# One SSD staging buffer at another address of the arena: over RWKV head pairs 3 and 4 instead of over pairs 5 to 7

## The chip, the cores and the metric

The kernel runs on one core of a Trainium2 chip. The metric is the device time of one execution in microseconds (us). The times and the profile are of the hardware. TensorE is called PE here, its weight loads PEld, VectorE DVE, ScalarE ACT, GpSimd POOL, and SyncE, which issues most of the loads, SP.

## The reference

One layer over 256 tokens of width 1024, in float32:

```
h = LN(x)
z, xbc, dt, f_rwkv, f_hgrn, gates = split(h @ w_in)
y_a = SSD(z, conv(xbc), dt)        16 heads of 64, 2 groups, state 128, chunks of 64
y_b = RWKV7(f_rwkv)                16 heads of 64, delta-rule state
y_c = HGRN2(f_hgrn)                8 heads of 128
m   = sum_i sigmoid(gate_i) * (y_i @ w_br_i)
h   = LN(alpha*h + m @ w_out)
h   = LN(alpha*h + MoE(h))         16 experts of 512, top 2 of one group of 4
```

For the SSD, the columns x, b and c of xbc are convolved along time and go through SiLU. Then, for each group, the products of c and b over the tokens are multiplied by decay factors, and these weights are multiplied with x.

## The kernel before

The 256 tokens are held as two tiles of 128. All of the mixers' scratch lies in one SBUF tile, the *arena*, of 122 KB on each partition. A `Bump` hands out pieces of it between two addresses in KB, and a named piece is a ring of buffers that is used over and over. Nothing is copied or freed when a stage takes over addresses of an earlier one: the program puts a wait on whatever read or wrote these bytes last. A scheduler orders the instructions of each engine when the program is built, by its own model of durations and by which instruction could start; every engine then runs its list strictly in that order. A different address can so change the order on all engines.

The stages, as the program writes them:

- `rwkv_part` and `rwkv_a` prepare the RWKV heads in pairs p = 0 to 7. Pair p keeps its chunk matrices at 8 + 9.5p KB: first `bkt` (2 KB), `uv` (2 KB), `sc` (4 KB), `ars` (1.5 KB). Pair 3 lies at 36.5 to 46, pair 4 at 46 to 55.5, pair 5 at 55.5 to 65, pair 6 at 65 to 74.5, pair 7 at 74.5 to 84.
- `rwkv_b` runs the recurrence over four chunks for two pairs at a time, in four rounds j = 0 to 3; round 3 is pairs 6 and 7. One chunk is a chain of small matmuls (L654, L658, L662, L670) with ACT copies between them, and the round ends with L687 and L691, which read `uv`, `sc` and `ars` for the last time. Then follow a group norm on DVE (L694 to L708), transposes (L717) and the output (L722 to L724). `hgrn(j)` stands beside each round; its last transposes are L920, of what ACT writes in L917.
- `feat` multiplies the normalized input with 256 columns of `w_in`. `stream` loads the weights by SP into `raw`, splits them on ACT (`whi`, L183) and DVE (`wlo`, L184) into two parts, and PE runs 48 matmuls of 128x256 (L366, L367, L368), 12 for one split tile; four split tiles can be ahead of PE. These *streams* are most of PE's work, and the scheduler puts them between the small matmuls. A stream with `yhi`, `ylo` instead of `hhi`, `hlo` is that of a branch, whose input y is split by the same two lines.
- `ssd_prep` convolves b and c (`conv`, L928 to L933) into `bcm`, with the ring `cth` as scratch, and multiplies them (L1003, L1004) into the products `cb` of the two groups.
- `ssd_weights(g)` loads the decay sums `ab` by a DMA that POOL issues (L1020), for token tile 0 and, into the same buffer, for tile 1. ACT makes `wdg` of each with eight Relus (L1029) and an Exp (L1031), and `woff` of the second with an Exp (L1023); DVE multiplies them by `cb` (L1032, L1024).
- `ssd` transposes x (L1064), scales it on DVE (L1067, L1069) and multiplies with the three weights: L1073 with `wdg` of tile 0, L1075 with `wdg` of tile 1, L1077 with `woff`.
- `branches`, `router` and `moe` follow. The MoE weights are loaded by SP into slots of the arena as these come free.

Of the kernel before, what the change touches and what calls it, by code (L numbers as in the profile page):

```python
# [139 lines left out]
class Kern:  # L140
# [847 lines left out]
    def ssd_prep(self):  # L988

        nc, A = self.nc, self.A  # L990
        mp = self.pmm
        a = self.sda = Bump(self.ar, 64, 102)
        bcm = a.new([128, 4, L])
        for m in range(2):
            ps = self.feat(COL_B + m * 256)
            for f in range(2):
                th = a.new([128, L], "cth", 2)
                self.conv(ps[:, f, :], 8 + 2 * m + f, bcm[:, 2 * m + f, :], th)
        self.gates(range(NG - NZ - NY, NG - NZ))
        self.cbs = []  # L1000
        for g in range(2):
            cps = mp.tile([128, 3, 128], F32, name="mm")
            nc.tensor.matmul(cps[:, 0:2, :], bcm[:, g, 0:128], bcm[:, 2 + g, :], start=True, stop=True)  # L1003
            nc.tensor.matmul(cps[:, 2, :], bcm[:, g, 128:256], bcm[:, 2 + g, 128:256], start=True, stop=True)  # L1004
            cb = a.new([128, 3, 128])
            nc.vector.tensor_tensor(cb[:, 0:3:2, :], cps[:, 0:3:2, :],
                                    self.tri[:, None, :].to_broadcast([128, 2, 128]), op=OP.mult)
            nc.scalar.activation(cb[:, 1, :], cps[:, 1, :], AF.Copy)
            self.cbs.append(cb)
# [721 lines left out]
```

## Time and profile before

| what | value |
|---|---|
| median of 3 runs | 830.43 us (830.31 to 831.64) |
| profiled execution | 829.69 us |
| span of that execution, first to last instruction | 827.9 us |
| PE busy | 784.8 us, 95% of the span |
| DVE, ACT, POOL busy | 510.1, 369.7, 134.7 us |
| mean granted clock of PE | 0.977 of full speed |

The profiled execution is 0.7 us below the median of the runs. A busy share of an engine is the time in which at least one of its instructions ran; the time between the span and the execution's time (1.8 us) lies before the first and after the last instruction.

### The profile page before, as it was taken

How to read it: one execution, taken by the hardware profiler on the slowest of the kernel's cores; microseconds unless marked ns; L12 is line 12 of the kernel's file. 1: busy time of each engine (PE TensorE's matmuls, PEld its weight loads, DVE VectorE, ACT ScalarE, POOL GpSimd, SP SyncE). 2: the span in 40 equal slices, each digit the busy share in tenths (PEclk: the TensorE clock that was granted, in tenths of full speed). 3: DMA queues.
4: the chain of work that ended last, by engine and by line, in shares of the span. 5: the costliest groups of instructions: out<-in, count | busy, mean ns of one | idle time of the engine just before them, and what ended most of it. 6: DMA issues, size and time to landing. Idle time of an engine off the chain costs nothing. (4 is left out here: it accounts for less than half of the span.)

```text
span 827.9 us, 16484 instructions
## 1 busy us (share of the span) xinstructions
PE 784.8 (95%) x6354; PEld 604.5 (73%) x6354; DVE 510.1 (62%) x1150; ACT 369.7 (45%) x824; POOL 134.7 (16%) x204
## 2 busy tenths in 40 slices
PE   7999969999999999999998999999999999999991
PEld 5898859988898899898797999999444434443440
DVE  6897669999997555567579887785611111111136
ACT  3755445574645555645477755453412121211111
POOL 3364614450102001102002111000000000001201
PEclk9999969999999999999899999999999999999996
DMA  7544564575445455366179568985999999999941
GB/s 229 177 118 114 50 161 119 140 180 155 107 132 148 128 155 153 103 203 193 38 237 299 178 205 283 349 271 161 390 386 386 387 387 386 387 386 386 386 179 54
DMA packets 146526, 183.93 MB, mean 222 GB/s; under 512 B 25609, under 2 KB 94472, under 8 KB 146440
## 3 DMA queue, kind: packets, MB, share of 16 engines
q1 hardware_dynamic: 142888, 176.91, 65.3%
q0 software_dynamic: 1504, 3.20, 2.2%
q10 hardware_dynamic: 2048, 2.70, 1.0%
q8 instruction: 52, 0.85, 0.4%
q14 instruction: 34, 0.28, 0.1%
HBM read 180.12 MB, written 2.65 MB: 221 GB/s over the span
## 5 line engine op out<-in xcount | busy, mean ns | idle before, releaser
L183 ACT ACTIVATE whi<-raw 128x512 fp32r<-128x512 f32 x268 | 165.5, 623 | 162.9 <-PE st L367 126.3
L184 DVE TENSOR_TENSOR wlo<-raw,whi 128x512 fp32r<-128x512 f32 x268 | 189.1, 715 | 77.3 <-ACT whi L183 64.2
L368 PE MATMUL st<-hhi,wlo 128*128 128x256 f32 (+1 forms) x744 | 212.0, 293 | 9.0 <-DVE wlo L184 8.8
L366 PE MATMUL st<-hhi,whi 128*128 128x256 f32 (+1 forms) x744 | 210.0, 290 | 2.2 <-ACT arena L784 1.4
L367 PE MATMUL st<-hlo,whi 128*128 128x256 f32 (+1 forms) x744 | 208.4, 288 | 0.0
L368 PEld LDWEIGHTS st<-hhi,wlo 128*128 128x128 f32 (+1 forms) x744 | 140.3, 192 | 16.6 <-DVE wlo L184 10.8
L366 PEld LDWEIGHTS st<-hhi,whi 128*128 128x128 f32 (+1 forms) x744 | 140.5, 192 | 7.1 <-issue 2.6
L367 PEld LDWEIGHTS st<-hlo,whi 128*128 128x128 f32 (+1 forms) x744 | 140.3, 192 | 3.1 <-issue 1.6
L1445 PE MATMUL b<-arena,xg 128*64 128x512 f32 x288 | 78.8, 596 | 0.0
L367 PE MATMUL st<-ylo,whi 128*128 128x256 f32 x192 | 53.8, 288 | 1.5 <-DVE ylo L184 1.5
L366 PE MATMUL st<-yhi,whi 128*128 128x256 f32 x192 | 53.9, 287 | 0.0
L368 PE MATMUL st<-yhi,wlo 128*128 128x256 f32 x192 | 53.1, 287 | 0.4 <-DVE wlo L184 0.2
L1445 PEld LDWEIGHTS b<-arena,xg 128*64 128x64 f32 x288 | 23.9, 137 | 38.0 <-issue 34.5
L1515 DVE SCALAR_TENSOR_TENSOR elo<-b,egs,ehi 128x512 fp32r<-128x512 f32 x15 | 11.3, 750 | 60.7 <-ACT ehi L1514 60.7
L1495 PE MATMUL b<-arena,ehT 128*64 128x512 f32 x144 | 43.0, 596 | 0.0
L367 PEld LDWEIGHTS st<-ylo,whi 128*128 128x128 f32 x192 | 36.4, 192 | 2.1 <-DVE ylo L184 1.7
L368 PEld LDWEIGHTS st<-yhi,wlo 128*128 128x128 f32 x192 | 36.2, 193 | 1.0 <-DVE wlo L184 0.8
L366 PEld LDWEIGHTS st<-yhi,whi 128*128 128x128 f32 x192 | 36.5, 192 | 0.3 <-ACT yhi L183 0.2
L1360 POOL TENSOR_TENSOR arena<-arena 128x512 f32<-128x512 bf16 x4 | 4.5, 1158 | 197.2 <-PE b L1445 197.2
L1484 ACT ACTIVATE ehT<-b 128x256 f32<-128x256 f32 x16 | 6.2, 389 | 67.7 <-PE b L1483 67.7
L1476 DVE SCALAR_TENSOR_TENSOR ehi<-ehi,b 128x256 f32<-128x256 f32 x16 | 6.0, 418 | 47.2 <-PE b L1445 47.2
L593 DVE TENSOR_TENSOR arena<-arena 128x1 f32<-128x1 f32 (+15 forms) x64 | 34.0, 531 | 0.8
(448 smaller groups left out, 1431.0 us busy)
## 6 DMA issues: line engine op xcount, KB each, us to landing
raw<-in_w_in_dram SPq DMA_DIRECT2D x102, 512.0 KB, 3.8
arena<-in_exp_w_gate_dram SPq DMA_DIRECT2D x40, 512.0 KB, 10.8
arena<-in_exp_w_down_dram SPq DMA_DIRECT2D x34, 512.0 KB, 10.8
arena<-in_exp_w_up_dram SPq DMA_DIRECT2D x32, 512.0 KB, 10.8
xsl<-in_exp_w_up_dram SPq DMA_DIRECT2D x32, 512.0 KB, 10.8
xsl<-in_exp_w_down_dram SPq DMA_DIRECT2D x20, 512.0 KB, 10.8
xsr<-in_exp_w_gate_dram SPq DMA_DIRECT2D x16, 512.0 KB, 10.8
raw<-in_w_br_rwkv_dram SPq DMA_DIRECT2D x8, 512.0 KB, 4.0
```

The costliest lines, as they stand in the source:

```text
L183: nc.scalar.activation(hi, raw, AF.Copy)
L184: nc.vector.tensor_tensor(lo, raw, hi.bitcast(F32), op=OP.subtract)
L366: nc.tensor.matmul(o, hi[:, kq, fs], xhi[:, k, :], start=st and f == 0, stop=False)
L367: nc.tensor.matmul(o, hi[:, kq, fs], xlo[:, k, :], start=False, stop=False)
L368: nc.tensor.matmul(o, lo[:, kq, fs], xhi[:, k, :], start=False, stop=sp and f == nf - 1)
L593: nc.vector.tensor_tensor(po, tu[:, :n, :t + 1], eu[:, :t + 1, t][:, None, :].to_broadcast([128, n, t + 1]), op=OP.mult)
L1360: nc.gpsimd.tensor_tensor(o, x[1], x[2], op=OP.add)
L1445: nc.tensor.matmul(ps[hs[e]], xg[:, k, hs[e]], W[nm, e, k // 2][:, k % 2, :], start=k == 0, stop=k == KT - 1)
L1476: nc.vector.scalar_tensor_tensor(th[:, c], th[:, c], 0.5, q["pu"][:, c], op0=OP.mult, op1=OP.mult)
L1484: nc.scalar.activation(q["hT"][:, 2 * j:2 * j + 2], tp, AF.Copy)
L1495: nc.tensor.matmul(pd[hs[e], :], q["hT"][:, k, hs[e]], W["exp_w_down", e, (n, k // 2)][:, k % 2, :], start=k == 0, stop=k == 3)
L1515: nc.vector.scalar_tensor_tensor(lo, pd, q["gs"], hi.bitcast(F32), op0=OP.mult, op1=OP.subtract)
```

## The change

`bcm`, `cth` and the two `cb` are taken from a Bump at 40 to 49 KB (9 KB are exactly what they need). They had come from the SSD's Bump at 64 KB, in which everything that `ssd_weights` and `ssd` take after them now moves down: `ab` from 73 to 64, the first `wdg` from 77 to 68, `woff` from 81 to 72, the second `wdg` from 85 to 76. `ssd` takes its own `cth` from that Bump.

```diff
@@ -989,7 +989,8 @@
 
         nc, A = self.nc, self.A
         mp = self.pmm
-        a = self.sda = Bump(self.ar, 64, 102)
+        self.sda = Bump(self.ar, 64, 102)
+        a = Bump(self.ar, 40, 49)
         bcm = a.new([128, 4, L])
         for m in range(2):
             ps = self.feat(COL_B + m * 256)
```

The added line moves every later line of the file down by one, so that L1020 of before is L1021 now, and so on. The order of the instructions changes from round 1 of the recurrence on. Three places matter below.

On PE, in round 3 of the recurrence (pairs 6 and 7), before: the second chunk follows the first, and the third the second, with no stream between.

```order
L368 MATMUL st<-hhi,wlo 128x256
L654 MATMUL ch<-arena 64x64 x2
L658 MATMUL ch<-arena 64x64 x2
L654 MATMUL ch<-arena 64x64 x2
L658 MATMUL ch<-arena 64x64 x2
L662 MATMUL ch<-arena 64x64 x4
L670 MATMUL ch<-arena 64x64 x4
```

The same place on PE now, up to the first streams behind that step; 19 stream matmuls stand there before the chunk's L662.

```order
L654 MATMUL ch<-arena 64x64 x2
L658 MATMUL ch<-arena 64x64 x2
L654 MATMUL ch<-arena 64x64 x2
L658 MATMUL ch<-arena 64x64 x2
L368 MATMUL st<-hhi,wlo 128x256
L366 MATMUL st<-hhi,whi 128x256 x2
L367 MATMUL st<-hlo,whi 128x256 x2
```

Streams stand now between all the steps of round 3. When the last L691 of round 3 is reached, PE has 2098 stream matmuls behind it before the change and 2197 now, of 3192 in all; the other matmuls up to there are as many (831 before it in both).

On PE, behind that last L691, now: 35 stream matmuls (not shown), and then the head of the SSD.

```order
L715 MATMUL ch<-arena 128x256 x2
L920 MATMUL mm<-ident,hr 128x128
L1004 MATMUL mm<-arena 128x256
L1005 MATMUL mm<-arena 128x128
L920 MATMUL mm<-ident,hr 128x128
L717 MATMUL ch<-ident,arena 128x128 x4
L920 MATMUL mm<-ident,hr 128x128 x2
L1004 MATMUL mm<-arena 128x256
L1005 MATMUL mm<-arena 128x128
L1065 MATMUL mm<-ident,arena 128x128 x2
L366 MATMUL st<-yhi,whi 128x256
L1074 MATMUL mm<-arena 64x128 x2
```

Two more L1065, 12 stream matmuls of the branch, and the ten matmuls L1076, L1078, L1074, L1076, L1078 follow at once. Before the change, 169 stream matmuls stand between the last L691 and the last of these ten; now 48 do. PE has 2267 stream matmuls behind it at that last matmul (L1077 before, L1078 now) before the change and 2245 now.

On ACT, at the same place, now: the group norm's squares (L703), the last two splits for the 35 streams, and then the SSD's weights in one run.

```order
L703 ACTIVATE arena<-arena 128x256 x2
L183 ACTIVATE whi<-raw 128x512
L932 ACTIVATE arena<-arena 128x256
L928 ACTIVATE arena<-st,hcb,hcw 128x256
L183 ACTIVATE whi<-raw 128x512
L1030 ACTIVATE arena<-arena,sdT 128x128 x8
L1032 ACTIVATE arena<-arena 128x1024
L932 ACTIVATE arena<-arena 128x256
L917 ACTIVATE hr<-mm,hr_y 128x128 x4
L1024 ACTIVATE arena<-arena 128x1024
L1030 ACTIVATE arena<-arena,sdT 128x128 x8
L1009 ACTIVATE arena<-mm 128x128
```

Two L722, the first split of the branch's input (`yhi`), and the Exp L1032 of the second `wdg` come next. Before the change, eight splits of stream weights stood between the first Relu and that Exp; now none does.

## Rows read from the trace of the kernel before

**Rows 1.** Busy time of each engine over the span (page, part 1).

```profile
PE 784.8 (95%) x6354; PEld 604.5 (73%) x6354; DVE 510.1 (62%) x1150; ACT 369.7 (45%) x824; POOL 134.7 (16%) x204
```

**Rows 2.** Granted clock of PE in 40 slices, tenths of full speed (page, part 2).

```profile
PEclk9999969999999999999899999999999999999996
```

**Rows 3.** Stretches: length, busy time (instructions) by engine, PEclk, DMA share, GB/s.

```profile
399.60:404.90 5.30, 3.38 (x54) 2.29 (x52) 4.37 (x13) 4.16 (x18) 0.00 (x0) 1.00 0.37 102
404.90:411.70 6.80, 6.66 (x41) 5.88 (x41) 4.50 (x12) 1.81 (x5) 0.00 (x0) 0.50 0.01 1
...
419.86:438.99 19.13, 19.13 (x156) 18.87 (x156) 16.60 (x51) 16.60 (x43) 3.49 (x4) 1.00 0.80 249
438.99:449.90 10.91, 8.32 (x65) 7.11 (x63) 10.05 (x19) 8.21 (x18) 1.43 (x2) 0.84 1.05 354
...
102.30:110.70 8.40, 0.03 (x1) 0.03 (x2) 2.15 (x6) 0.14 (x1) 0.00 (x0) 0.63 0.71 152
110.70:118.10 7.40, 7.40 (x48) 5.86 (x49) 7.23 (x24) 5.58 (x14) 2.84 (x5) 0.50 0.64 173
...
456.00:570.00 114.00, 113.60 (x972) 110.74 (x970) 91.22 (x184) 63.32 (x119) 8.25 (x12) 1.00 0.78 253
590.00:800.00 210.00, 210.00 (x1279) 89.50 (x1277) 43.25 (x94) 40.19 (x96) 8.96 (x8) 1.00 1.03 379
```

**Rows 4.** PE in order of time, round 3: start, length, instruction [idle before, releaser].

```profile
401.21 0.45 PE L662 MATMUL ch<-arena 64*64 64x64 f32 x8 [0.76 <-ACT arena L660]
```

**Rows 5.** PE in order of time: streams at half and at full clock.

```profile
407.64 0.41 PE L366 MATMUL st<-hhi,whi 128*128 128x256 f32 x1
407.86 0.41 PE L367 MATMUL st<-hlo,whi 128*128 128x256 f32 x1
...
422.29 0.28 PE L366 MATMUL st<-hhi,whi 128*128 128x256 f32 x1
422.41 0.28 PE L367 MATMUL st<-hlo,whi 128*128 128x256 f32 x1
```

**Rows 6.** PE in order of time: end of round 3, head of the SSD.

```profile
417.84 0.69 PE L687 MATMUL ch<-arena 128*64 128x64 f32 x16
...
419.26 0.60 PE L691 MATMUL ch<-arena 128*64 128x128 f32 x5
...
440.44 0.44 PE L1073 MATMUL mm<-arena 128*64 128x128 f32 x4 [1.07 <-ACT yhi L183]
...
442.88 0.58 PE L367 MATMUL st<-ylo,whi 128*128 128x256 f32 x1 [1.52 <-DVE ylo L184]
...
449.65 0.39 PE L1077 MATMUL mm<-arena 128*64 128x128 f32 x4
```

**Rows 7.** The loads of `ab`: POOL in order of time, and landing times of line L1020.

```profile
419.91 1.00 POOL L1020 DMA_DIRECT2D arena<-acsd  x1 [32.65 <-ACT arena L932]
430.29 0.90 POOL L1020 DMA_DIRECT2D arena<-acsd  x1 [9.38 <-ACT whi L183]
...
DMA to landing us min/median/max: 4.5/6.0/7.4
```

**Rows 8.** ACT in order of time, the SSD's weights.

```profile
427.29 2.46 ACT L1029 ACTIVATE arena<-arena,sdT 128x128 f32<-128x128 f32 x8 [1.64 <-DMA arena<-acsd]
...
430.96 1.05 ACT L1031 ACTIVATE arena<-arena 128x1024 f32<-128x1024 f32 x1
...
434.92 1.06 ACT L1023 ACTIVATE arena<-arena 128x1024 f32<-128x1024 f32 x1
...
436.45 0.56 ACT L722 ACTIVATE arena<-ch,par 128x256 f32<-128x256 f32 x1
...
439.79 1.68 ACT L183 ACTIVATE yhi<-arena 128x512 fp32r<-128x512 f32 x3
```

**Rows 9.** DVE in order of time, scaling of x and the second `wdg`.

```profile
442.75 0.41 DVE L1067 TENSOR_TENSOR arena<-mm,sdT 128x256 f32<-128x256 f32 x1
...
445.69 1.22 DVE L1032 TENSOR_TENSOR arena<-arena 128x1024 f32<-128x1024 f32 x1
```

## The prediction

> **What bounds the kernel now.** I read the busy times first: PE runs for 784.8 of 827.9 us [rows 1], and every other engine far less. So I looked for where PE stands still or runs slowly, since only that can change: both kernels issue the same matmuls. The granted clock [rows 2] is below full speed in a few slices. The stretches [rows 3] then say what lies where. From 456 to 570 us PE is busy for 113.60 of 114.00 us, and in the MoE, from 590 to 800, for all of 210: there is nothing to win or to hide in. What can move lies between 399 and 456 us, where the recurrence ends and the SSD begins:
>
> - 399.6 to 404.9: PE works 3.38 of 5.30 us. These are the two chunks of round 3 without streams between them; PE waits for ACT copies, 0.76 us the longest time [rows 4]. 1.9 us are lost.
> - 404.9 to 411.7: the clock is 0.50, which is 1.2 instead of 2.4 GHz, for 6.8 us [rows 3]. Streams start 0.22 us apart instead of 0.12 [rows 5]. That costs half of 6.8, 3.4 us.
> - 419.9 is the end of the last L691 [rows 6]; I call this moment T. From T to 439.0 PE is never idle, because 19 us of streams lie under the preparation of the SSD weights [rows 3].
> - 439.0 to 449.9: PE is busy for 8.32 of 10.91 us at a clock of 0.84. The two waits in it are 1.07 and 1.52 us [rows 6]. The last L1077 ends at 450.0, which is T + 30.1.
>
> **What the change adds and takes away.** The convolutions no longer wait for pairs 6 and 7, so their streams go ahead of T. That has a good side and a bad one, and I price both up to the last of the ten matmuls at the head of the SSD, and from there on.
>
> *Before T.* 99 more stream matmuls lie ahead of T, at 0.12 us each [rows 5] 11.9 us. They fill the gaps of round 3: the idle 1.9 us go, and with them, I take it, the slow clock that followed, 3.4 us. T becomes 419.9 + 11.9 - 1.9 - 3.4 = 426.5. If the gaps stay as they are, it is up to 1.9 us later.
>
> *From T on.* The work that lay under the SSD weights is now behind PE. PE has 35 stream matmuls, 4.2 us, and then stands in its list before matmuls that need ACT's L917, the branch's `yhi` and the two `wdg`. What sets these is a chain that could not start earlier than before: `ab` lies now at 64 to 68 KB, over `bkt` and half of `uv` of pair 6. Both are last read in round 3, `uv` by the first group of L687, which I put 1.2 us ahead of T (the two pairs' L687 and L691 take 2.0 us together, from 417.84 on [rows 6], and the first group is a good quarter of them). So the move freed bcm and cb of pairs 6 and 7, but not `ab`. In us after T:
>
> - load of `ab` for tile 0, issued at -1.2, used 7.4 later, as at 427.29 after 419.91 [rows 7, 8]: 6.2
> - eight Relus, 2.46 [rows 8]: 8.7
> - second load into the same buffer, issued 0.5 after the last Relu as before, used 4.6 later (430.29 to 434.92 [rows 7, 8]): 13.8. Meanwhile ACT runs the first Exp, 1.05 [rows 8], and L917, which are done before the load lands.
> - Exp of `woff` and eight Relus, 1.0 + 2.5: 17.3
> - L1009 and two L722, 0.2 + 2 x 0.56: 18.6; first `yhi`, a third of 1.68: 19.1; second Exp, 1.05: 20.2 [rows 8]
> - DVE's product, 1.22, then L724 and the scaling of the second x, 0.41 + 0.7 [rows 9]; L724 is priced like L1067 there, and the smaller half of the scaling at 0.3: 22.5
> - the last matmuls: 23.5.
>
> Every link is queued on ACT behind the one before it, and behind them all stand the next splits of stream weights, so that PE cannot run other streams either: four split tiles are all that is ahead. So PE stands for about half of these 23.5 us. The head of the SSD ends at 426.5 + 23.5 = 450.0, where it ended before. But 22 stream matmuls fewer are behind PE by then: 2.6 us more are left to do.
>
> *The clock.* After the 8.4 us in which PE stood from 102.3 on, the clock was 0.50 for another 7.4 us of work [rows 3], which cost 3.7 us. The new stand is longer, and I take 3.7 for it. The two bounds: after the 2.6 us of waits at 440 the slow part was about 3.5 us long (0.16 x 2 x 10.91 [rows 3]), which cost 1.7; and nothing, if the clock is back when the streams resume.
>
> *What costs nothing.* PE has 113.6 of 114.0 us of work in the part that follows, and the MoE's loads are issued at nearly the same place of SP's list (the 14th expert load stands behind 108 stream loads before, 111 now; the 23rd behind 120 in both). Waits of ACT's own loads (rows of x and of the layer norm over the old `bcm` and `cb`) stand among splits that run up to four tiles ahead of PE, 5.7 us; a load that lands as late as 7.4 us after its issue would show 1.7 of them on PE. The later `cb` reader and the first slots that were free earlier change no wait on PE.
>
> **The sum**: 0.0 at the head of the SSD, 2.6 for the streams left, 3.7 for the clock: 6.3 us on the profiled execution's 829.69, 836.0. The runs' median is 0.74 above that execution, so 836.7.
>
> One rule speaks about the loads. The trace gives 7.4 and 4.6 us for the two that the sum uses, 512 KB each, and 4.5 to 7.4 over all four [rows 7]. The Trainium skill (DMA: Bandwidth & Descriptors, section "Anatomy of one DMA — SWDGE (gpsimd) path") has a fixed cost of about 2.0 us plus the bytes at 436 GB/s, from which I estimate 3.2 us for such a load; the trace does not agree, since its shortest takes 4.5. By that page's price the sum would be 3.8 us instead of 6.3; I keep the rows.
>
> **Rivals.**
>
> 1. *The loads are short.* If both land at the shortest time in the trace, 4.5 us, the Relus start at T + 5.1 instead of 6.2 (not earlier: ACT's last split waits for the 35 streams, 4.2, and takes 0.6 with some 0.3 for the signals), and the second load saves 0.1. That is 5.1 us slower, 835.5, and each us by which the second is shorter still takes off one more. For it: SP has few loads to issue while the splits stand still, and the first load's 7.4 fell into a stretch with a DMA share of 0.80 [rows 3]. Against it: only one of the two moves the sum. The rule of the Trainium skill's DMA page named above would be this rival.
> 2. *The clock is not lost.* If PE's scattered matmuls keep the clock up, or it is back when the streams resume, 3.7 go: 2.6 slower, 833.0. Against it: three stands, of 8.4, 1.9 and 2.6 us, all were followed by 0.50.
> 3. *Faster: the chain from T is much shorter.* The gain ahead of T, 5.3 us, is real in all cases; the loss is the chain. At 17.2 us instead of 23.5 the two are even, below 15.5 the kernel is faster: at 14, some 3 us, 827.2. For it: before the change the same links were pulled apart by other work on ACT (16.60 of 19.13 us busy [rows 3]), so their true length was never seen in one piece. Against it: with both loads at 4.5 and the Relus from 5.1 on, the links still add up to 22.
> 4. *No change*: the chain is around 17 us, or the branch's streams can run under it; 830.4.
>
> **Chances.** The forecast 0.55; rival 1 0.09 and rival 2 0.10, both slower too; rival 4 0.12; rival 3 0.14. What this kernel can tell from no change is about 0.2%, 1.7 us. So slower by more: 0.74, within: 0.12, faster by more: 0.14. The range: on the low side the first load at its minimum (-1.1) and no loss of clock (-3.7) give +1.5, 831.9; on the high side a second load of 7.4 (+2.8) and gaps that stay (+1.9) give +11.0, 841.4. That is the forecast's own range. To leave out no more than two in ten I take it down to 829.5, into rival 4; the faster case and some of what lies above stay out.
>
> **What will show it.** PE busy through round 3 with a clock of 1.00 there; the last L691 near 426; then PE idle for some 12 us in the next 24, with waits named after L917, `yhi` and the DVE products; ACT waiting for the `ab` loads; a clock of 0.50 for several us after it; the last L1078 near 450; from there to the end the old distance plus about 6 us. I am wrong if round 3 keeps its gaps, if L1078 comes within 17 us of the last L691, or if PE's waits behind T are short because something else than this chain releases them.

## The result and the profile after

The changed kernel takes 838.43 us (838.25 to 839.58, 4 runs); the kernel before took 830.71 us (830.31 to 831.64, 4 runs) beside it. The ratio on record is 1.0086, with a 95% interval from 1.0067 to 1.0104; the two medians alone give 1.0093, 7.7 us slower, where 6.3 were forecast. The profiled execution took 839.58 us, with a span of 837.8 us. Its span is 9.9 us longer than that of before, more than the medians differ, since the one lies above its median and the other below.

Busy times and granted clock of the kernel after (page, parts 1 and 2), for [rows 1, 2]:

```profile
PE 787.3 (94%) x6354; PEld 606.0 (72%) x6354; DVE 510.9 (61%) x1150; ACT 370.2 (44%) x824; POOL 133.9 (16%) x204
...
PEclk9999979999999999999987999999999999999996
```

Every engine has the same work as before to within 2.5 us. The reduced clock, which stood in slice 20 before, stands now in slices 21 and 22. Four stretches say more (length, busy time of PE, PEld, DVE, ACT and POOL, granted clock, DMA share, GB/s): from 330 us to T, the 35 us from T on, from there to the first matmul of the MoE, and the MoE. T is the end of the last L691, as in the prediction. First the kernel before:

```profile
330.00:419.86 89.86, 86.29 (x817) 75.08 (x815) 56.11 (x130) 45.51 (x122) 8.87 (x7) 0.96 0.46 140
419.86:454.86 35.00, 31.54 (x249) 29.82 (x249) 31.61 (x79) 28.32 (x68) 7.53 (x8) 0.95 0.87 282
454.86:586.20 131.34, 128.84 (x1070) 122.91 (x1069) 102.39 (x240) 69.83 (x130) 8.25 (x12) 1.00 0.76 248
586.20:810.91 224.71, 223.60 (x1348) 96.72 (x1348) 51.14 (x111) 42.67 (x101) 8.96 (x8) 1.00 0.98 361
```

The same four stretches after, and the piece of the second in which the clock was down:

```profile
330.00:426.25 96.25, 96.25 (x914) 84.71 (x914) 57.55 (x137) 51.62 (x136) 8.48 (x8) 1.00 0.44 128
426.25:461.25 35.00, 25.27 (x174) 23.11 (x174) 27.70 (x73) 23.84 (x58) 6.10 (x8) 0.76 0.72 234
461.25:596.08 134.83, 128.41 (x1047) 121.68 (x1046) 104.93 (x239) 68.73 (x127) 9.31 (x12) 0.99 0.79 260
596.08:820.77 224.69, 223.58 (x1348) 96.71 (x1348) 51.13 (x111) 42.66 (x101) 8.94 (x8) 1.00 0.97 357
434.20:451.30 17.10, 10.06 (x45) 8.53 (x47) 11.47 (x32) 12.44 (x31) 3.68 (x4) 0.50 0.62 201
```

Up to T, PE is now busy for all of 96.25 us at full clock. T itself comes 6.4 us later, because 99 more streams lie ahead of it. From T to the MoE, 99 streams fewer are to be run, 11.9 us of work, and yet this stretch did not become shorter: 166.34 us before, 169.83 us after. PE's idle time in it rose from 5.96 to 16.15 us (the lengths less the busy times). The MoE is unchanged. So the 9.9 us are 6.4 ahead of T and 3.5 behind it.

PE in order of time (start, length, instruction, [idle before, what ended it]): T, the head of the SSD and one place behind it, for [rows 6].

```profile
425.65 0.60 PE L691 MATMUL ch<-arena 128*64 128x128 f32 x5
...
438.70 0.47 PE L920 MATMUL mm<-ident,hr 128*128 128x128 f32 x1 [7.20 <-ACT hr L917]
...
446.20 0.58 PE L366 MATMUL st<-yhi,whi 128*128 128x256 f32 x1 [2.54 <-ACT yhi L183]
...
451.79 0.39 PE L1078 MATMUL mm<-arena 128*64 128x128 f32 x4
...
508.92 0.71 PE L1090 MATMUL ch<-ones,arena 128*128 128x1 f32 x4 [2.82 <-POOL arena L1086]
```

Behind T, PE waits 7.20 and 2.54 us, first for L917 and then for `yhi`; the head ends at 452.18, T + 25.9. The wait at 506 us was not foreseen. The loads on POOL for [rows 7], then ACT for [rows 8], then DVE, each in order of time:

```profile
425.50 1.00 POOL L1021 DMA_DIRECT2D arena<-acsd  x1 [42.78 <-ACT whi L183]
436.30 0.90 POOL L1021 DMA_DIRECT2D arena<-acsd  x1 [9.79 <-ACT arena L1030]
```

```profile
433.31 2.44 ACT L1030 ACTIVATE arena<-arena,sdT 128x128 f32<-128x128 f32 x8 [2.11 <-DMA arena<-acsd]
...
436.74 0.40 ACT L932 ACTIVATE arena<-arena 128x256 f32<-128x256 f32 x1
438.28 1.14 ACT L917 ACTIVATE hr<-mm,hr_y 128x128 f32<-128x128 f32 x4 [1.14 <-DVE hr_y L177]
441.17 1.06 ACT L1024 ACTIVATE arena<-arena 128x1024 f32<-128x1024 f32 x1 [1.74 <-DMA arena<-acsd]
...
445.52 0.62 ACT L183 ACTIVATE yhi<-arena 128x512 fp32r<-128x512 f32 x1
```

```profile
437.17 0.43 DVE L933 SCALAR_TENSOR_TENSOR arena<-arena 128x256 f32<-128x256 f32 x1 [2.45 <-ACT arena L932]
```

Read together: the first load is used 7.8 us after its issue, the second 4.9. ACT's list holds the Relus and an Exp ahead of a convolution's tanh, L932. DVE waits 2.45 us for that tanh at L933, and behind it in DVE's list stand the small steps of the reciprocal root for L917. So the late first load reached PE through a convolution and a norm, which the forecast had as done meanwhile.

### The profile page after: what moved, and what is told of

Same layout as the page of the kernel before. It is cut to its first block, busy times and chain, and to the rows that moved or that the text cites. A ratio compares the mean times of both kernels' runs of the same rounds, so it can differ in the third digit from the quotient of the medians.

```text
span 837.8 us, 16475 instructions
## 1 busy us (share of the span) xinstructions
PE 787.3 (94%) x6354; PEld 606.0 (72%) x6354; DVE 510.9 (61%) x1150; ACT 370.2 (44%) x824; POOL 133.9 (16%) x204
## 5 line engine op out<-in xcount | busy, mean ns | idle before, releaser
L367 PEld LDWEIGHTS st<-hlo,whi 128*128 128x128 f32 (+1 forms) x744 | 138.6, 190 | 3.1 <-issue 1.5
```

Of the source, the lines that this page charges most:

```text
L367: nc.tensor.matmul(o, hi[:, kq, fs], xlo[:, k, :], start=False, stop=False)
```

## The experiments

The comparison in each is with runs of the kernel before on the same chip; 1.0086 is what the changed kernel has. Streams ahead of T are counted in the order of the program, T, the length from T to the MoE and PE's idle time in it come from the profiled execution, one for each run.

| run | ratio to before (95%) | streams ahead of T | T, us | T to MoE, us | PE idle in it, us |
|---|---|---|---|---|---|
| before | 1 | 2098 | 419.86 | 166.34 | 5.96 |
| e10_zz3 | 0.9996 (0.9974 to 1.0018) | 2098 | 418.82 | 166.38 | 7.62 |
| e11_sx4 | 1.0045 (1.0027 to 1.0063) | 2098 | 419.24 | 173.11 | 9.90 |
| e4_weights_early | 1.0069 (1.0050 to 1.0089) | 2088 | 417.39 | 176.94 | 11.01 |
| e9_z_held | 1.0046 (1.0021 to 1.0070) | 2088 | 413.46 | 177.82 | 12.10 |
| e2_c_conv_held | 1.0039 (1.0025 to 1.0054) | 2136 | 419.53 | 173.95 | 12.97 |
| changed kernel | 1.0086 (1.0067 to 1.0104) | 2197 | 426.25 | 169.83 | 16.15 |
| e7_late_split_held | 1.0103 (1.0084 to 1.0123) | 2197 | 427.81 | 168.52 | 15.40 |
| e6_norm_first | 1.0125 (1.0103 to 1.0147) | 2197 | 426.22 | 172.69 | 16.34 |
| e5_both_ab_early | 1.0096 (1.0073 to 1.0118) | 2184 | 426.66 | 170.65 | 16.87 |
| e1_ab_early | 1.0102 (1.0081 to 1.0123) | 2197 | 427.11 | 173.02 | 16.93 |
| e12_zz3_on_changed | 1.0141 (1.0113 to 1.0169) | 2197 | 427.12 | 173.10 | 17.08 |
| e8_filler_matmuls | 1.0111 (1.0089 to 1.0134) | 2197 | 425.91 | 169.41 | 11.58, and 7.2 of filler |
| e3_conv_moved_alone | 1.0116 (1.0090 to 1.0142) | 2213 | 424.54 | 174.97 | 19.10 |

The heads are not alike, so the times at which they end do not compare by themselves. Between T and the last of the ten matmuls PE runs 48 streams in the changed kernel, 60 in e1, 96 in e5, 83 in e6, 59 in e8, 110 in e3, 123 in e2, and 169 or 170 in the kernel before, e4 and e9. (The 97 and 145 in the expectations of e2, e4 and e9 reach only to the first of the two groups of L1078.) The edits add a few lines to the file, so some line numbers in the traces below are a little higher than in the changed kernel.

**Are the loads the chain?** In e1 the first load is moved off the path, in e5 both.

```diff
-        self.sda = Bump(self.ar, 64, 102)
+        self.sda = Bump(self.ar, 68, 102)
+        self.sdb = Bump(self.ar, 49, 53)
...
-            ab = t8("ab")
+            ab = self.sdb.new([128, 8, 128], "ab")
```

> The changed kernel with one more address changed: ab lies at 49 to 53 KB, free since round 2, so its first load can land before round 3 ends; every other buffer stays where the changed kernel has it. My theory (the stand behind the last L691 is the chain of the two loads into one buffer, the Relus and the Exps): the first Relu starts within 0.5 us of the last L691 instead of 7.1 us behind it, the last matmul of the head comes some 19 us behind the last L691 instead of 25.9, and 12 stream matmuls fewer are left (1.4 us): about 830 us, 8 below the changed kernel. Rival (the stand is set by the group norm and the branch's yhi, and by the slow clock; the loads are only beside it): 836 to 839 us, the last matmul of the head still 24 us or more behind the last L691.

Measured 841.28 us against 831.79 for before. The first Relu started 1.4 us ahead of T, but the last matmul of the head came at T + 28.2 and nothing was gained. The second load was used 7.7 us after its issue in this run, and ACT stood 3.3 us for it. So one load alone proved nothing, and e5 takes both away:

```diff
-            ab = t8("ab")
+            ab = t8("ab") if g else self.ar.at(49 - 13 * t, [128, 8, 128])
```

> The changed kernel with the two ab of the first group in two buffers that are free before round 3 ends (49 to 53 and 36 to 40 KB); all other addresses as in the changed kernel. Neither load is late any more. New theory (two chains share ACT's list behind the last L691, the SSD's weights and the group norm that leads to yhi; 8.7 us of Relus, Exps and splits stand ahead of L703 here, so yhi still comes 17 to 18 us behind the last L691): the stand stays about as long, 835 to 838 us. Theory of the prediction (the two loads are the chain): the head ends 8 to 10 us earlier, 829 to 831 us.

Measured 839.32 us against 831.44. This edit did more than its expectation says: the Bump still starts at 64 KB, and the first group now takes no `ab` from it, so its weights and all that follows them lie 4 KB lower than in the changed kernel, the first `wdg` at 64 instead of 68. The order is another one too, with 2184 streams ahead of T. ACT of e5, its last Relus and the first `yhi`:

```profile
427.19 1.26 ACT L1030 ACTIVATE arena<-arena,sdT 128x128 f32<-128x128 f32 x4
...
442.97 1.16 ACT L183 ACTIVATE yhi<-arena 128x512 fp32r<-128x512 f32 x2 [0.25 <-DVE yc L921]
```

PE of e5, the end of round 3, the waits behind it and the end of the head:

```profile
426.06 0.60 PE L691 MATMUL ch<-arena 128*64 128x128 f32 x5
428.00 1.10 PE L715 MATMUL ch<-arena 128*128 128x256 f32 x4 [1.34 <-DVE arena L702]
433.37 0.58 PE L366 MATMUL st<-hhi,whi 128*128 128x256 f32 x1 [4.27 <-DVE arena L1057]
...
446.98 0.39 PE L367 MATMUL st<-ylo,whi 128*128 128x256 f32 x1 [2.41 <-DVE ylo L184]
...
454.73 0.39 PE L1078 MATMUL mm<-arena 128*64 128x128 f32 x4
```

The Relus are through 1.8 us behind T, no wait names a load, and PE stands all the same: for the group norm's L702, for a PSUM bank that DVE's L1057 has to empty, for `ylo`. The head ends at T + 28.5, with 48 streams more in it than in the changed kernel, and from T to the MoE PE is idle for 16.87 us where it was 16.15. So the time is not lost by the loads alone: with both done, other chains took their place. How much of that is the 4 KB and the new order is not shown.

**Which chain goes first.** e6 keeps both loads early, gives the weights the addresses of the changed kernel again (`ab` of the second group gets 64 to 68 KB for itself), and queues the Relus of the first group on ACT behind the last L722 (`l722`).

```diff
-        self.sda = Bump(self.ar, 64, 102)
+        self.sda, self.sdb = Bump(self.ar, 68, 102), Bump(self.ar, 64, 68)
...
-            ab = t8("ab")
+            ab = self.sdb.new([128, 8, 128], "ab") if g else self.ar.at(49 - 13 * t, [128, 8, 128])
...
             for h in range(8):
+              with (self.tc.issue_after(self.l722.ins) if g == 0 else ExitStack()):
                 nc.scalar.activation(w[:, h, :], ab[:, h, :], AF.Relu, scale=-1.0,
```

> As the run before (both loads early), and all Relus of the first group are queued on ACT behind the last L722, so that the group norm goes first. New theory: yhi comes 10 to 12 us behind the last L691 instead of 19.3, PE stands for 4 to 5 us there instead of 9.7, and the weights, whose loads are done, are ready when the 31 streams behind yhi are through: 831 to 834 us. Rival (the weights are the longer chain whatever goes first): PE stands as long, only later, before the matmuls with the weights: 836 us or more.

Measured 842.06 us, against 831.44. DVE and ACT of e6:

```profile
436.11 0.69 DVE L708 TENSOR_TENSOR arena<-arena,gr_y 128x512 f32<-128x512 f32 x1
```

```profile
444.62 1.66 ACT L183 ACTIVATE yhi<-arena 128x512 fp32r<-128x512 f32 x3
```

The norm's last step on DVE starts only at T + 9.9 even now, with eleven steps of convolutions among its steps, and the Relus took their turn ahead of `yhi`, which came at T + 18.4. My 10 to 12 us were wrong; the rival's number came out.

**Half of the change, and its opposite.** e3 keeps `ab` and all behind it at the addresses of before; the order then puts the norm first by itself.

```diff
-        self.sda = Bump(self.ar, 64, 102)
+        self.sda = Bump(self.ar, 73, 102)
```

> Only the first half of the change: bcm, cth and cb at 40 to 49 KB, ab and what follows at their addresses of before (ab at 73 KB). The order puts yhi and 91 streams of the branch ahead of the second and third weights. My theory: round 3 is filled, PE stands for 7 us behind the last L691 until yhi comes, and the slow clock adds 2 to 3 us: 831 to 833 us, between the two kernels. Rival (moving b and c makes the whole loss, the place of ab none of it): 837 to 839 us. Other rival (the shift of ab and the weights makes the whole loss): 826 us, the gain ahead of the last L691 alone.

Measured 842.61 us, against 831.79. The places in e3 where PE waits, behind T (total, times, longest):

```profile
PE st L366 <- DVE arena L1135: 5.4, 2, 5.0
PE ch L1090 <- POOL arena L1086: 5.1, 2, 4.5
...
PE mm L920 <- ACT hr L917: 2.9, 1, 2.9
PE st L366 <- ACT yhi L183: 2.4, 1, 2.4
```

The head was what I expected: two waits of 2.9 and 2.4 us, and `yhi` 11.7 us behind T instead of 19.3. But 4.5 us were lost at 455 us and 5.0 at 504 us, and the total is no better. The total lies above all three ranges and is nearest to the first rival: moving b and c alone costs at least as much as the whole change. e4 is the opposite move, from the kernel before: the weights early, b and c where they were.

```diff
+        self.sdb, self.sdw = Bump(self.ar, 49, 53), Bump(self.ar, 40, 48)
...
-            ab = t8("ab")
+            ab = self.sdb.new([128, 8, 128], "ab")
...
-            w = t8("wdg%d" % t)
+            w = self.sdw.new([128, 8, 128], "wdg%d" % t)
```

> The opposite move, from the kernel before: b, c and cb stay at 64 to 73 KB, and ab (49 to 53 KB) and the two wdg (40 to 48 KB) go to addresses that are free before round 3. The Relus and Exps then stand ahead of the last L691 on ACT, and 145 streams are between it and the head's last matmul. My theory: round 3 keeps its gaps and its slow clock (5.3 us), but the waits of 2.6 us and the slow clock at the head of the SSD go (4.3 us): 826 to 828 us, faster than both. Rival (the weights were hidden under the streams before and are not on the path): 830 to 831 us.

Measured 837.98 us, against 831.79: slower, by neither theory. The Relus and Exps of both `wdg` were done at 386 us, 31 us ahead of T, and PE still waited 3.48 us for `yhi` at T + 20.8. PE, ACT and DVE of e4 at this wait:

```profile
441.64 0.58 PE L366 MATMUL st<-yhi,whi 128*128 128x256 f32 x1 [3.48 <-ACT yhi L183]
```

```profile
440.96 1.67 ACT L183 ACTIVATE yhi<-arena 128x512 fp32r<-128x512 f32 x3 [2.83 <-DVE yc L921]
```

```profile
437.45 2.88 DVE L1033 TENSOR_TENSOR arena<-arena 128x1024 f32<-128x1024 f32 x2
440.25 0.68 DVE L921 TENSOR_TENSOR yc<-mm,hr 128x512 f32<-128x512 f32 x1
```

The profile names L921 as what `yhi` waited for, the last product of `hgrn`, and in DVE's list L921 stands behind both products L1033 of the weights with `cb`. Only the ACT half of the weights was early; `cb` comes from b and c, which this run leaves where they were.

**Streams kept back.** With all addresses of the changed kernel, e2 holds the convolutions of c on ACT behind the last `uv` copy of round 3 (`uv3`), and e9 the first z columns on PE behind the last L691 (`l691`).

```diff
...
-                self.conv(ps[:, f, :], 8 + 2 * m + f, bcm[:, 2 * m + f, :], th)
+                with (self.tc.issue_after(self.uv3.ins) if m else ExitStack()):
+                    self.conv(ps[:, f, :], 8 + 2 * m + f, bcm[:, 2 * m + f, :], th)
```

> The changed kernel, all addresses kept, but the two convolutions of c are queued on ACT behind the last uv copy of round 3, so that their PSUM banks hold the streams back: 2136 stream matmuls ahead of the last L691 (2098 before the change, 2197 with it), 97 between it and the head's last matmul (169 and 48). My theory (what matters is how many streams are left to lie over the chain): the chain behind the last L691 stays at 24 to 26 us, but 11.6 us of it are covered, and most of round 3 is still filled: 829 to 832 us. Rival (the new addresses cost by themselves, in later loads into 40 to 49 KB or in the shifted weights): 837 to 839 us.

```diff
...
-                ps = self.feat(COL_Z + (2 * g + m) * 256, other=ZCH)
+                with (self.tc.issue_after(self.l691.ins) if g + m == 0 else ExitStack()):
+                    ps = self.feat(COL_Z + (2 * g + m) * 256, other=ZCH)
```

> The changed kernel, all addresses kept; the streams of the first z columns are queued on PE behind the last L691. So 2088 stream matmuls lie ahead of it (before the change 2098, with it 2197), and 145 lie between it and the head's last matmul (169 and 48). Theory (the streams that need nothing of the recurrence are the cover of what follows the last L691; the change spends them ahead of it): PE's idle time and half-clock loss in the 35 us behind the last L691 fall from 14.9 us (changed kernel) to at most 7 (before: 4.9), round 3 has its gaps and its slow clock again, and with the later waits of the changed kernel the whole takes 833 to 836 us. Rival (the new addresses make the loss, whatever lies over it): 838 us or more, with 12 us or more lost there.

Measured 835.73 us against 831.79, and 834.60 against 831.37. Both lie between the two kernels: about half of the loss comes back, and both intervals lie below 1.0086, that of e9 just touching the changed kernel's (1.0070 and 1.0067). So the new addresses by themselves do not make the whole loss. That it is the number of streams spent ahead of T which counts fits both runs, but each hold changes the order as well, and e2 met neither its theory's range nor its rival's. The theory's details failed too: e9 lost 8.0 us of idle time in the 35 us behind T, not 7 at most with the slow clock, since `yhi` came 27.7 us behind its early T.

**The clock.** e8 puts 16 matmuls, whose result nothing reads, where PE stood.

```diff
+        if p > 5:
+            for _ in range(8):
+                nc.tensor.matmul(fps[:, 0], self.ones, self.ones[:, None, :].to_broadcast([128, 2, 128]),
+                                 start=True, stop=True)
         for c2 in range(2):
```

> The changed kernel with 16 matmuls added (128x256, ones by ones, into the PSUM area that the transposes L717 write afterwards), behind the L715 of pairs 6 and 7: about 7 us of work in the place where PE stood for 7.2 us. Nothing of the result changes. Theory (the slow clock behind the stand is part of the price): the granted clock stays at 1.00 up to the head, and 2 to 4 us come back: 834 to 836 us. Rival (the chain sets the end of the head and the slow clock lies inside it): the clock stays up, the time stays at 838.

The 35 us behind T of e8, and a wait of PE in them:

```profile
425.91:460.91 35.00, 29.05 (x201) 26.01 (x201) 27.80 (x72) 24.03 (x58) 7.92 (x8) 0.90 0.71 230
```

```profile
446.83 0.70 PE L1078 MATMUL mm<-arena 128*64 128x128 f32 x4 [4.99 <-DVE arena L1072]
```

The mean clock of the 35 us rose from 0.76 to 0.90, and the time did not fall: 840.11 us, against 831.44. PE now stood 4.99 us for a scaling of x on DVE instead (L1072, which is L1068 of the changed kernel). So the higher clock was not worth anything in this run; as 59 streams instead of 48 lie in its head, the order is not quite the same, and the clock alone is not set apart.

**The waits behind the head.** e7 takes the cause of the wait at 506 us away.

```diff
...
-                for k in range(0, KT, 2):
+                with ExitStack() as es:
+                  if i == 1:
+                    es.enter_context(self.tc.issue_after(self.hold[0].ins))
+                    es.enter_context(self.tc.issue_after(self.hold[1].ins))
+                  for k in range(0, KT, 2):
```

> The changed kernel, all addresses kept; only the split of the second branch's input (yhi on ACT, ylo on DVE) is queued behind L1080 and L1084 of the sixth head pair of the SSD. In the changed kernel L1080 stood 2.4 us behind four such ylo on DVE, and PE then waited 2.8 us at 506 us for L1086 and ran at half clock for 3.4 us. Theory (this second stand belongs to the loss, and comes from the order of DVE and ACT there): the wait at 506 us goes and some 4 us with it, 834 us. Rival (the second stand only repeats time that is lost anyway, because the streams left over are too few): another wait of the same length appears behind it, 837 to 839 us.

PE of e7, at that place:

```profile
508.24 0.39 PE L366 MATMUL st<-yhi,whi 128*128 128x256 f32 x1 [2.28 <-ACT yhi L183]
...
509.75 0.40 PE L367 MATMUL st<-ylo,whi 128*128 128x256 f32 x1 [0.78 <-DVE ylo L184]
```

One wait of 2.82 us went and two came, 2.28 and 0.78 us, for the very split that was held: 839.82 us, against 831.44, as the rival had it. The last three runs ask whether any other order costs as much. e10 and e11 give the kernel before a buffer more, which changes the order behind the head and hardly ahead of it; e12 gives it to the changed kernel.

```diff
-                    zz = a.new([128, L], "zz", 2)
+                    zz = a.new([128, L], "zz", 3)
```

> The kernel before with a third buffer for zz (1 KB more; xt moves up by it), no work added or taken away. The order is the same up to the head of the SSD and differs behind it: the four matmul groups for the norm (msq) stand at 2307, 2419, 2630 and 2766 stream matmuls instead of 2306, 2424, 2591 and 2730. Theory (any other order behind the head costs some us in late waits of the SSD's second half, the term that the prediction missed; the changed kernel's 5 us there are not of its addresses): same losses up to the head, 3 to 5 us more behind it, 833 to 836 us. Rival (the late waits come from what the change does ahead of the head): 830 to 831 us.

In e11 it is a buffer for `sx` instead:

```diff
-                    x = a.new([128, L], "sx", 3)
+                    x = a.new([128, L], "sx", 4)
```

> The kernel before with a fourth buffer for sx (1 KB more; cth, zz and xt move up by it), a second order of the same work: same up to the head, msq at 2316, 2435, 2618 and 2751 stream matmuls. Theory as in the run before: 2 to 5 us more behind the head, 833 to 836 us. Rival: 830 to 831 us.

Measured 831.02 and 835.17 us, against 831.37. From T to the MoE, e10 and then e11, and the longest wait of PE there in e11:

```profile
418.82:585.20 166.38, 158.76 (x1318) 151.50 (x1317) 134.76 (x320) 98.23 (x198) 19.57 (x23) 1.00 0.79 260
```

```profile
419.24:592.35 173.11, 163.21 (x1316) 155.38 (x1317) 135.11 (x320) 98.16 (x198) 17.17 (x23) 0.97 0.76 246
```

```profile
526.55 0.39 PE L368 MATMUL st<-yhi,wlo 128*128 128x256 f32 x1 [4.12 <-DVE wlo L184]
```

e10 takes the same time as before, so that not every other order costs something. e11 has a stand of 4.12 us at 522 us and is 0.45% slower, with the same work and, on PE, the same order up to the head. An order can cost this much without any part of the change.

> The changed kernel with the third buffer for zz that cost nothing on the kernel before. Up to the head of the SSD the order on PE and ACT is that of the changed kernel but for one Exp ahead of yhi; behind it the group of streams ahead of the third msq is 48 long instead of 22, where the changed kernel waited 2.8 us at 506 us. Theory (the change costs 8 us up to the head's end and the gain ahead of the last L691 pays for most; the other 5 us, in the stage behind, are of the order there and not of the addresses): the losses behind the last L691 stay at 13 to 15 us, those from 35 us behind it to the MoE fall from 8.0 to about 3 to 4, and the time to 833 to 835 us. Rival (that stage loses its 8 us in any order, since the change leaves too few streams for it): 838 us again.

Measured 842.28 us, against 831.81. PE of e12, at the head and behind it:

```profile
439.58 0.47 PE L920 MATMUL mm<-ident,hr 128*128 128x128 f32 x1 [7.20 <-ACT hr L917]
...
544.66 0.68 PE L366 MATMUL st<-yhi,whi 128*128 128x256 f32 x2 [2.10 <-ACT yhi L183]
```

The first wait of the head is the same 7.20 us, the wait at 506 us is gone, and another of 2.10 us stands at 543 us. What cost nothing on the kernel before did not help the changed one; the rival was right that nothing comes back, and the run is even slower than its 838. None of the twelve beats the kernel before; e10 equals it.

## Why the prediction was right, and where its steps failed

**Ahead of T: right.** T was put at 426.5 and came at 426.25, PE was busy through round 3, and the slow clock of [rows 3] was gone.

**A stand of PE behind T: right.** 12 us of idle time were forecast in 24 us, with waits for L917 and `yhi`; there were 9.7 us in 25.9, under these names. A wait for the DVE products did not show at the head.

**What sets its length: wrong in part.** The step was that the head is set by "a chain that could not start earlier than before", load, Relus, load, Relus. In the changed kernel its links came out nearly as priced: the second load was used at T + 14.9 for 13.8, the first `yhi` was done at T + 19.9 for 19.1, the head ended at T + 25.9 for 23.5. But with both loads gone (e5), the head ended no sooner, if with 48 streams more in it, and with the Relus and Exps done 31 us ahead of T (e4), PE waited for `yhi` too. The loads are one of several chains of about this length that run side by side in the in-order lists of ACT and DVE: the weights, their products with `cb`, the two norms (L702 to L722 and L917 to L921), the convolutions. Taking one away left the next. The cause that the runs favour is the one beside it in the same step: the work that lay over these chains had been moved ahead of T. In the table, PE's idle time from T to the MoE grows with the streams spent ahead of T, from 6 to 12 us at 2088 to 2098 over 13 at 2136 to 15 to 19 at 2184 to 2213, filler counted as idle. That is a trend and not a proof: within 10 streams it varies by 6 us, and e4 and e9, with 10 streams fewer ahead of T than before, do not have the time of before either.

**The clock: a term in the wrong place.** 3.7 us were added for streams at half clock behind the head. The half clock lay from 434.2 to 451.3 us, inside the head, and the streams right behind the head ran at full clock. What it cost inside the head stays open: e8 got nothing back from a higher clock, but in the changed kernel PE never stood from the end of its wait for `yhi` to the end of the head, at a mean clock of 0.58, and the head ended 2.4 us later than priced.

```profile
446.20:452.18 5.98, 5.98 (x40) 5.03 (x40) 5.98 (x13) 3.59 (x7) 1.56 (x2) 0.58 1.01 324
```


**The streams left over: right in the trace.** 22 streams more are left to PE at the head's end than before, 2.6 us.

**"What costs nothing": missed 5.1 us.** From the head's end to the MoE, the changed kernel took 143.9 us (596.08 less 452.18), before 136.2 (586.20 less 450.04). The two stretches, before and then after:

```profile
450.04:586.20 136.16, 132.79 (x1100) 126.68 (x1100) 107.21 (x250) 73.34 (x137) 10.86 (x15) 1.00 0.76 248
```

```profile
452.18:596.08 143.90, 137.48 (x1122) 130.75 (x1122) 112.36 (x254) 75.09 (x143) 11.49 (x15) 0.99 0.78 258
```

2.6 of these 7.7 are the streams left over. Of the other 5.1, 3.0 are more idle time of PE (6.42 us after, 3.37 before), the 2.82 us at 506 us first, 1.7 are the cost of 3.4 us at half clock right behind that wait, and 0.4 I can't place. The step that failed is the reason given for this term: PE was busy for 113.6 of 114.0 us there in the kernel before, and I took it that the new order would keep it so. So the forecast of 0.0 + 2.6 + 3.7 was 2.1 + 2.6 + 5.1 in the profiled execution, with nothing for the clock right behind the head. That the total comes out near is in part luck: the 3.7 us of a term in the wrong place stand in for 7.2 us in two terms that were put at nothing.

**The rivals.** Short loads (1) would have made it 835.5: in e5 no wait names a load, and the time stayed. The rule of the Trainium skill that stood beside that rival (DMA: Bandwidth & Descriptors, "Anatomy of one DMA — SWDGE (gpsimd) path"; estimate 3.2 us) disagrees again: from issue to landing these loads took 4.8 to 7.8 us in the changed kernel. A clock that is not lost (2) held right behind the head, but the time did not come out lower by it. A much shorter chain (3) or no change (4) did not come.

**What stays open.** Which order of the lists would cover the chains with some 2200 streams ahead of T, or whether one exists: eight orders with 2184 to 2213 were run, and PE lost 15 us or more in each, with the filler counted as lost. And how much of the loss behind the head is of the change and how much of the order that happened to come out: e11 lost 3.8 us by order alone, and a stand of 1.7 to 5.0 us between 500 and 545 us is in the trace of every run but the kernel before and e10.

## What to carry to other kernels

Filling gaps with work from later is a gain only if the stretch that it is taken from becomes shorter. Look there first for chains on other engines that this work lies over: here 11.9 us of matmuls left a stretch of 166 us, which then took 170. And where several chains of like length run side by side in in-order lists, an experiment that removes one of them says little by itself; count the idle time of the whole stretch, since a wait that is taken away may stand elsewhere a few us on.

## What the runs showed of the hardware

The same POOL instruction took very different times beside different DVE work. The first L723 behind T took 0.74 us in the kernel before, and the two took 1.65 us each in e4, where DVE ran the two L1033 (shown with e4 above), which took 1.44 us each instead of the 1.22 of [rows 9]. POOL of e4, and the same two L1033 in e5, where POOL ran nothing beside all but the first 0.2 us of them:

```profile
437.61 3.31 POOL L723 TENSOR_TENSOR arena<-arena 128x256 f32<-128x256 f32 x2 [17.60 <-ACT arena L722]
```

```profile
443.57 2.42 DVE L1033 TENSOR_TENSOR arena<-arena 128x1024 f32<-128x1024 f32 x2
```

Both engines were slower while they ran together. The Trainium skill (SBUF — State Buffer, section "SBUF: two separate sides") says that a DVE operation with two SBUF inputs and a GpSimd operation that reads SBUF exclude each other. These rows agree in that both lost time; that one stands for the whole of the other they do not show, since the four instructions of e4 took 3.47 us together, from 437.45 to 440.92, and 3.92 us by the times that they took otherwise (2 x 0.74 + 2 x 1.22). POOL's spans are rough in the profile.

A load of the same 512 KB was first used between 4.9 and 8.9 us after its issue (4.9 and 7.8 in the changed kernel, 7.7 in e1, 8.9 in e3), with ACT waiting for it each time, so that no single price for it holds, not even within one kernel.
